# TensorE's task order in four planned stretches, taken from fixed permutations

## The chip, the cores and the metric

The kernel runs on one core of one Trainium2 chip. A core has a matrix engine (TensorE, in the profile PE for its matmuls and PEld for its weight loads), three engines for elementwise work (VectorE or DVE, ScalarE or ACT, GpSimd or POOL), and SyncE (SP), which here only issues the DMA transfers. Each engine runs its own instructions in the order in which they were issued, and waits on semaphores for the others. The metric is the device time of one execution in microseconds, the median of several runs.

## The reference

A two-layer encoder trunk is applied to two requests with shared weights: 256 and 512 tokens, each with the same 16 meta tokens in front, so 272 + 528 = 800 rows of 1024 numbers, all in float32. Layer 0 mixes tokens by multi-head latent attention, layer 1 by grouped-query attention in a window of 128 tokens with a sink logit for each head. Behind each follows a squared-ReLU MLP, and each of the four steps ends in a layer norm over a scaled residual:

```python
for i in range(DEPTH):                      # DEPTH = 2, DN_ALPHA = 4 ** 0.25
    mix = mla_mixer(h, ...) if i % 2 == 0 else gqa_mixer(h, ...)
    h = layer_norm(DN_ALPHA * h + mix, ln1_g[i], ln1_b[i])
    h = layer_norm(DN_ALPHA * h + sqrelu_mlp(h, mlp_w1[i], mlp_w2[i]), ln2_g[i], ln2_b[i])
return h[:, N_META:]

def sqrelu_mlp(x, w1, w2):                  # 1024 -> 4096 -> 1024
    h = jax.nn.relu(x @ w1)
    return (h * h) @ w2
```

`mla_mixer` has 16 heads with 64 plain and 32 rotated columns for queries and keys, and 64 for values; `gqa_mixer` has 16 query heads on 4 key heads of 64.

## The kernel before

Activations lie transposed, 128 of the 1024 features on the partitions and tokens along the free axis, in two halves of 400 tokens (`hf` 0 and 1; 384 of a half where the meta tokens are dropped). A float32 product is made of three matmuls: each operand is split into a rounded part (hi, by ScalarE) and the rest (lo, by VectorE), and `mm3` (lines 445 to 448) adds hi x hi, hi x lo and lo x hi in one PSUM bank. So each weight and each activation costs one ScalarE and one VectorE instruction before TensorE can use it. The MLPs use a seven-product scheme for blocks of two by two, whose sums of weights are made by VectorE or GpSimd (`weight_add`, line 1438).

After the input projection, which is written out in order, the work lies in four plans, built one after the other: attention 0 (`attention0`), MLP 0 (`mlp_middle` with l = 0), attention 1 (`attention1`) and MLP 1 (`mlp_middle` with l = 1). A plan is a list of tasks. Each has an engine, a planned cost in ns, a function that issues its instructions, what it reads and writes, and the buffers it holds (`Plan.task`). From them `Plan.order` makes the order in which all engines' instructions are issued:

- TensorE's tasks form a chain in the order in which the code writes them down: each depends on the one before (lines 238 to 240). That order is made by hand: which filling work stands between the scores of attention, how far transposes follow scores, and so on.
- For every task a latest start (`late`) is worked out back from the end, over dependencies and over buffers that have to come free, with `LAG` ns from one engine to another (190 behind TensorE, 70 behind VectorE and ScalarE, 90 behind GpSimd).
- `Plan.forward` then plays the plan forward: again and again it takes the task that can start first, or one on the same engine that is more urgent by `late`. For VectorE, ScalarE, GpSimd and SyncE this sets the order; for some sums it also chooses between GpSimd and VectorE (`ways`).
- Eight such rounds are made, each with `late` taken from the round before, and the round is kept whose last TensorE task ends first.

`Plan.issue` issues the tasks in the order of their planned starts. `plan.busy` says for how long other engines are still taken by the stretch before.

The two score banks of attention 0 (buffer `s`) are used in turn: `scores` (line 1045) fills one, VectorE takes the maximum (line 1060 or 1069), ScalarE the exponential (line 1064 or 1074), and then the bank is free. VectorE or GpSimd scales the result `p` (lines 1088 and 1091), `turn` (line 1110) transposes it on TensorE (line 1122), ScalarE copies it out (line 1129), `tmeta` does so for the meta keys (line 1139), and `avs` (line 1147) multiplies with the values. In attention 1 the same is done by `scores` (line 2185), `transposes` (line 2271; matmuls in lines 2283 and 2291, on the tiles `sma`), and `outputs` (line 2298). A layer norm is in three TensorE tasks: `mean`, `sums` (eight narrow matmuls, line 795 or 1524), then a square root on ScalarE and a reciprocal on VectorE (lines 799 and 800, or 1527 and 1528), and `scale` (line 805 or 1533), behind which VectorE and ScalarE scale and split the activations for what follows. In the MLPs `up_pair` and `down_group` write the products; each finished bank of a down product is added to `acc` by VectorE (line 1734). The last layer norm is in `end` (line 1875): `piece` writes the product and its addition (line 1906 or 1907), `norm` the statistics, the scaling and the output DMA.

The changed orders number TensorE's tasks of a plan from 0 as the code writes them down. The plans have 390, 360, 329 and 339 of them. Those that are spoken of below:

| plan | tasks |
|---|---|
| attention 0 | 7, 10, 13: the first scores (short request); 8 and 9: projections for the long request; 15, 18, 21, 24: scores of the long request; 16, 19, 22, 25: transposes (`turn`); 17 and 20: projections; 280, 328, 333: scores of the last two head pairs; 277, 279: `turn`; 282: a key projection; 305: first part of the output projection; 338, 339, 340: the last transposes; 341: the last `avs`; 342 to 349: parts of the output projection; 367, 370: `sums` and `scale` |
| MLP 0 | 1: `mean`; 8, 10 and 11: parts of up products; 9: `sums`; 12: `scale` |
| attention 1 | 14 and 16: `sums0` and `scale0`; 15: a down product that stands between; 33: `sums1`; 34: part of a query projection; 170, 171 and 178, 179: scores of block 5; 190 and 197: two transposes tasks on them; 175, 184: transposes and `outputs` of block 1 |
| MLP 1 | 1: `mean`; 9 and 12: `sums` and `scale`; 19 to 26: an up product in eight parts that follow the eight splits of the activations `hc`; 27 to 29: three up products; 32 to 34 and others: transposes of the residual; 327 to 338: `piece` |

## Time and profile before

| what | us |
|---|---|
| median of three runs | 1750.49 |
| lowest and highest | 1750.35 and 1751.98 |
| span of the profiled execution | 1750.74 |
| input projection, to TensorE's first planned task | 85.8 |
| attention 0, from TensorE's first task to that of MLP 0 | 373.5 |
| MLP 0 | 471.2 |
| attention 1 | 318.9 |
| MLP 1, to the last matmul's start | 493.2 |
| behind the last matmul | 8.1 |

The profiled execution's own time and the median differ by 0.25 us. The page of the profile gives each engine's busy time; the windows give the same for stretches of the span. A row of the timeline has a start (us from the span's start), a length, the engine and line, what is written and read, and, in brackets, how long the engine was idle before and what ended that. Consecutive instructions of one kind are merged with their count. A row of the waits names who waited for whom, the sum in us, how often, and the longest. Ends of matmuls are modelled: one starts before the one before it ends, so a busy TensorE isn't one at its peak.

### The profile page before, as it was taken

How to read it: one execution, taken by the hardware profiler on the slowest of the kernel's cores; microseconds unless marked ns; L12 is line 12 of the kernel's file. 1: busy time of each engine (PE TensorE's matmuls, PEld its weight loads, DVE VectorE, ACT ScalarE, POOL GpSimd, SP SyncE). 2: the span in 40 equal slices, each digit the busy share in tenths (PEclk: the TensorE clock that was granted, in tenths of full speed). 3: DMA queues.
4: the chain of work that ended last, by engine and by line, in shares of the span. 5: the costliest groups of instructions: out<-in, count | busy, mean ns of one | idle time of the engine just before them, and what ended most of it. 6: DMA issues, size and time to landing. Idle time of an engine off the chain costs nothing.

```text
span 1750.7 us, 28797 instructions
## 1 busy us (share of the span) xinstructions
PE 1732.5 (99%) x10806; PEld 1628.4 (93%) x10806; DVE 1448.0 (83%) x2937; ACT 1026.2 (59%) x2172; POOL 309.2 (18%) x290
## 2 busy tenths in 40 slices
PE   9999999999999999999999999999999999999998
PEld 9999999989999999999999998788989889988996
DVE  6998889886977898889876877876877888888877
ACT  5577777774655446545643627775665456545652
POOL 0011111112220111111103232332211111211110
PEclk9999999999999999999999999999999999999999
DMA  7211001114311221222122231021311222222222
GB/s 243 77 41 32 22 20 42 35 42 140 121 61 49 73 72 62 73 72 73 61 89 83 81 104 38 21 66 61 121 49 49 80 65 73 73 72 73 73 68 89
DMA packets 39453, 124.16 MB, mean 71 GB/s; under 512 B 4752, under 2 KB 9744, under 8 KB 39184
## 3 DMA queue, kind: packets, MB, share of 16 engines
q1 hardware_dynamic: 39312, 122.31, 21.3%
q8 instruction: 85, 1.39, 0.3%
q14 instruction: 56, 0.46, 0.1%
HBM read 119.15 MB, written 3.15 MB: 70 GB/s over the span
## 4 chain that ended last, share of the span: by engine, by line
PE 93%; DVE 4%; ACT 2%; issue 0%; DMA 0%; POOL 0%; SPq 0%; DVEq 0%; ACTq 0%
PE w L447 18%; PE w L448 18%; PE w L446 18%; PE wb L446 4%; PE wb L447 4%; PE wb L448 4%; PE wa L446 3%; PE wa L448 3%; PE wa L447 3%; PE wa L1155 2%; PE sa L446 2%; PE wa L1122 2%; PE wb L2309 2%; PE sa L448 2%; PE sa L447 2%; PE wb L2291 1%
## 5 line engine op out<-in xcount | busy, mean ns | idle before, releaser
L1734 DVE TENSOR_TENSOR acc<-acc,w 128x400 f32<-128x400 f32 (+1 forms) x306 | 184.3, 618 | 35.3 <-PE w L448 33.3
L1466 DVE TENSOR_TENSOR h<-sq,h 128x384 fp32r<-128x384 f32 (+1 forms) x164 | 94.6, 589 | 19.4 <-ACT h L1464 18.9
L446 PE MATMUL w<-h,wsp 128*128 128x400 f32 x316 | 108.9, 345 | 0.0
L447 PE MATMUL w<-h,wsp 128*128 128x400 f32 x316 | 108.9, 345 | 0.0
L447 PE MATMUL w<-h,wspi 128*128 128x400 f32 x316 | 108.9, 345 | 0.0
L446 PE MATMUL w<-h,wspi 128*128 128x400 f32 x316 | 108.7, 344 | 0.0
L448 PE MATMUL w<-h,wspi 128*128 128x400 f32 x316 | 108.7, 344 | 0.0
L448 PE MATMUL w<-h,wsp 128*128 128x400 f32 x316 | 108.6, 344 | 0.0
L1464 ACT CAST h<-sq 128x384 fp32r<-128x384 f32 (+1 forms) x164 | 82.5, 515 | 20.5 <-POOL sq L1472 19.3
L1091 POOL TENSOR_TENSOR p<-p,rs 106x512 f32<-106x512 f32 (+1 forms) x40 | 44.7, 1117 | 253.5 <-DVE pk L1082 162.2
L448 PE MATMUL w<-wspi,h 128*128 128x512 f32 (+1 forms) x182 | 71.6, 393 | 0.0
L446 PE MATMUL w<-wspi,h 128*128 128x512 f32 (+1 forms) x182 | 71.5, 393 | 0.0
L447 PE MATMUL w<-wspi,h 128*128 128x512 f32 (+1 forms) x182 | 71.5, 393 | 0.0
L1645 ACT COPY sq<-w 128x400 f32<-128x400 f32 (+1 forms) x72 | 35.0, 486 | 61.0 <-PE w L448 61.0
L1064 ACT ACTIVATE p<-sa,nm,rq 106x528 f32<-106x528 f32 (+1 forms) x80 | 63.4, 792 | 10.5 <-DVE nm L1061 4.5
L1060 DVE TENSOR_REDUCE nm<-sa 106x1 f32<-106x528 f32 (+1 forms) x80 | 56.3, 704 | 13.8 <-PE sa L448 12.4
L446 PE MATMUL w<-wsp,h 128*128 128x512 f32 (+1 forms) x170 | 67.1, 395 | 0.0
L448 PE MATMUL w<-wsp,h 128*128 128x512 f32 (+1 forms) x170 | 66.8, 393 | 0.0
L447 PE MATMUL w<-wsp,h 128*128 128x512 f32 (+1 forms) x170 | 66.7, 393 | 0.0
L446 PE MATMUL sa<-k,q 128*106 128x264 f32 (+5 forms) x208 | 63.8, 307 | 2.8 <-issue 0.9
L446 PE MATMUL w<-t,wsp 128*128 128x384 f32 (+1 forms) x176 | 60.0, 341 | 0.0
L448 PE MATMUL w<-t,wsp 128*128 128x384 f32 (+1 forms) x176 | 59.9, 341 | 0.0
(823 smaller groups left out, 6173.7 us busy)
## 6 DMA issues: line engine op xcount, KB each, us to landing
wrawo<-in_w_o_dram SPq DMA_DIRECT2D x32, 512.0 KB, 3.3
wraw0d<-in_w2b_dram SPq DMA_DIRECT2D x24, 512.0 KB, 3.3
wraw1d<-in_w2b_dram SPq DMA_DIRECT2D x18, 512.0 KB, 3.4
wrawq<-in_w_q_dram SPq DMA_DIRECT2D x8, 512.0 KB, 3.3
xr<-in_xT_dram SPq DMA_DIRECT2D x16, 200.0 KB, 3.4
wraw<-in_w_qn_dram SPq DMA_DIRECT2D x8, 384.0 KB, 3.1
wx1d<-in_w2b_dram SPq DMA_DIRECT2D x6, 512.0 KB, 3.2
out_dram<-fo SPq DMA_DIRECT2D x11, 256.0 KB, 2.0
```

Of the source, the lines that this page charges most:

```text
L446: nc.tensor.matmul(out, lh, rh, start=start, stop=False, **kw)
L447: nc.tensor.matmul(out, lh, rl, start=False, stop=False, **kw)
L448: nc.tensor.matmul(out, ll, rh, start=False, stop=stop, **kw)
L1060: plan.task("DVE", DVE(528), lambda: V.tensor_reduce(nm.t[:qm, 0:1], v(), axis=AX.XY, op=ALU.max, negate=True), reads=[ps], writes=[nm], n ...
L1064: lambda: S.activation(P_().rearrange("p (a b) -> p a b", b=264), v(), AF.Exp, bias=nm.t[:qm, 0:1], scale=sc, accum_out=rs.t[:qm, 0:1]),
L1091: f = lambda row=row, r=r, w=w: G.tensor_tensor(row()[:, META:T], row()[:, META:T], r().to_broadcast([qm, w]), ALU.mult)
L1122: nc.tensor.transpose(ps.t[:, k * qm : (k + 1) * qm], src[k], ident[:qm, :qm])
L1155: nc.tensor.matmul(av[64 * e : 64 * e + 64, :n], vt.t[:, k, h0 + 64 * e : h0 + 64 * e + 64], PT.t[:, e, k, :n], start=k == 0, stop=False, ...
L1464: plan.task("ACT", 530, lambda: S.copy(d.t[:, 0], c.t[:, :n]), reads=[c], writes=[(d, "hi")], new=[d])
L1466: "DVE", 570, lambda: V.tensor_tensor(d.t[:, 1], c.t[:, :n], d.t.bitcast(F32)[:, 0], ALU.subtract),
L1734: f = lambda: V.tensor_tensor(z, z, ps.t[:, : z.shape[-1]], ALU.add)
L2309: nc.tensor.matmul(av[64 * gi : 64 * gi + 64, :256], at["V"][:, kbs[k][0], gc : gc + 64], PT.t[:, a : a + 256], start=k == 0, stop=False, ...
```

## The change

TensorE's tasks keep what they do, and get another order: `ORDERS` has one permutation for each plan, by the numbers above, found beforehand by a local search. The chain of TensorE's tasks follows it. Against the order as written, 250 of 390, 308 of 360, 272 of 329 and 267 of 339 tasks stand at another place, by 1.3, 3.0, 2.3 and 2.2 places on average, and by 10, 24, 13 and 17 at most.

Three things go with it. Since a task can now depend on one with a higher number, the first `late` is worked out over a topological order in place of the numbers. Of the eight rounds that one is kept whose end is first, where an end now counts TensorE's last task and also the last task of each other engine, less a lead for each plan (`LEAD`; SyncE only where the lead is 0, in MLP 1). And in `end`, the small tiles of the last layer norm are made by whichever piece comes first. The orders of the other engines, and the issues of the DMAs, come from the same planner as before.

Of `ORDERS`, the lines that are spoken of below:

```diff
+import heapq
 import math
 from contextlib import ExitStack
 from types import SimpleNamespace
@@ -88,6 +89,51 @@
 DOWN_ORDERS = ((7, 1, 6, 5, 3, 4, 2), (1, 7, 6, 5, 3, 2, 4))
 
 
+ORDERS = [
+    "0 4 3 1 6 5 2 8-9 7 11-12 10 13-15 18 21 20 17 22 24-25 16 23 19 27 26 29 28 30 32-33 31 35 37 34 36 38-44 46-49 52 50-51 53 55 45"
...
+    "265-268 270 269 271 264 272-279 282 280-281 283 285-286 284 288 287 289 294 291-292 295 293 296 298 297 299-300 290 303 302 304 "
+    "301 308 307 306 305 313 310 309 315 311 314 317 316 318-319 312 320-321 323-326 322 327-330 332 331 334 337 333 336 338 335 339 "
+    "344 343 340 345 349 346 342 341 347-348 353 351-352 350 355 354 356-357 359-361 364 369 358 362 371 363 365-368 370 372 374-376 "
...
+    "0-1 5 2-4 10 6 11 7 9 8 12 15 13 16-17 19 18 20-21 14 22-25 29 26-28 30-31 36 33 37 41 32 39 34-35 46 38 40 45 47-48 53 50 43 49 "
...
+    "0-2 5 3-4 6-10 13 12 11 14 16-17 15 20 19 18 22 21 24 23 26 25 27-29 32 30-31 34 33 38 42 36 35 43-44 39 37 50-51 46 45 40 47 54 "
...
+    "178-179 177 174 180 183 175 181-182 184 186 185 190 188 187 191 196 192-194 197 195 189 199-203 198 207-208 210 209 205 211 206 "
...
+    "0-3 5 4 6-10 12 11 15-16 32 19 17 13 20-21 18 22 33 14 23-25 34 28-29 27 26 37 39 38 30 40 35 41 44 36 49-50 43 31 42 45 51-52 61 "
...
+    "309 313-314 319 316 308 320-321 315 324 322 318 323 317 326 325 327 329 328 330-331 333 332 335 334 337 336 338",
+]
+
+
+LEAD = (1400, 3000, 1400, 0)
+
+
 class Held:
 
 
@@ -102,10 +148,11 @@
 
     LAG = {"PE": 190, "DVE": 70, "ACT": 70, "POOL": 90, "SP": 0}
 
-    last = {}
+    last, count = {}, 0
 
     def __init__(self, bufs, own, in_turn=()):
         self.bufs, self.own, self.tasks, self.last, self.ways = bufs, own, [], {}, []
+        self.no, Plan.count = Plan.count, Plan.count + 1
 
         self.free = set(own) - set(in_turn)
         self.given = {tag: [] for tag in bufs}
@@ -162,7 +209,7 @@
 
 
         tasks, n = self.tasks, len(self.tasks)
-        line = [i for i in range(n) if tasks[i][0] == "PE"]
+        line = list(self.line)
         done, begin, places, took = {}, {}, [], {}
         ready = {i: 0.0 for i in range(n) if not deps[i]}
         wait = [len(d) for d in deps]
@@ -207,7 +254,7 @@
             e, cost, _ = self.ways[i][way[i]]
             held, port = tasks[i][4], tasks[i][5]
             if e == "PE":
-                line.pop(0)
+                assert line.pop(0) == i
             del ready[i]
             begin[i], done[i] = t, t + cost
             took[i] = way[i]
@@ -236,6 +283,10 @@
         tasks, n = self.tasks, len(self.tasks)
         deps = [set(t[3]) for t in tasks]
         line = [i for i in range(n) if tasks[i][0] == "PE"]
+        if ORDERS[self.no]:
+            ranks = [range(int(a), int(b or a) + 1) for a, _, b in (x.partition("-") for x in ORDERS[self.no].split())]
+            line = [line[k] for r in ranks for k in r]
+        self.line = line
         for a, b in zip(line, line[1:]):
             deps[b].add(a)
         after = [[] for _ in range(n)]
@@ -255,15 +306,28 @@
                 for i in users[id(x)]:
                     if i < k:
                         turns[i].append(k)
+        wait = [len(d) for d in deps]
+        heap = [i for i in range(n) if not wait[i]]
+        place = {}
+        while heap:
+            i = heapq.heappop(heap)
+            place[i] = len(place)
+            for k in after[i]:
+                wait[k] -= 1
+                if wait[k] == 0:
+                    heapq.heappush(heap, k)
+        assert len(place) == n
         late = [0.0] * n
-        for i in reversed(range(n)):
-            late[i] = min([late[k] - self.lag(i, k) for k in after[i] + turns[i]], default=0.0) - tasks[i][1]
+        for i in sorted(place, key=place.get, reverse=True):
+            later = [k for k in after[i] + turns[i] if place[k] > place[i]]
+            late[i] = min([late[k] - self.lag(i, k) for k in later], default=0.0) - tasks[i][1]
         first = min(late)
         late = [x - first for x in late]
         best = None
         for _ in range(rounds):
             begin, at, places, took = self.forward(deps, after, late)
-            end = max(begin[i] + tasks[i][1] for i in begin if tasks[i][0] == "PE")
+            ends = {e: max((begin[i] + self.ways[i][took[i]][1] for i in begin if self.ways[i][took[i]][0] == e), default=0.0) for e in self.LAG}
+            end = max(ends["PE"], *(ends[e] - LEAD[self.no] for e in ends if e != "SP" or not LEAD[self.no]))
             if best is None or end < best[0]:
                 best = (end, begin, at, took)
 
@@ -1900,7 +1964,7 @@
                 plan.task("PE", 12 * (229 if w == 512 else 119), run, reads=reads, writes=[ps], new=[ps])
 
                 def add():
-                    if i == 0:
+                    if not tl:
                         make()
                     if through:
                         return V.tensor_tensor(z[:, c], z[:, c], ps.t[:, :w], ALU.add)
@@ -2587,6 +2651,7 @@
 
     arrays = _layout({k: np.asarray(v) for k, v in inputs.items()})
     arrays.update(_constants())
+    Plan.last, Plan.count = {}, 0
     nc = bacc.Bacc("TRN2", target_bir_lowering=False, num_devices=1, dynamic_dma_scratch_size=1024)
     feed, ins = {}, {}
     for name, a in arrays.items():
```

## The prediction

> **What bounds the kernel now.** I read the page first, then the stretches between the four plans, then TensorE's waits, then the timeline around the longest of them.

> ```profile
> span 1750.7 us, 28797 instructions
> PE 1732.5 (99%) x10806; PEld 1628.4 (93%) x10806; DVE 1448.0 (83%) x2937; ACT 1026.2 (59%) x2172; POOL 309.2 (18%) x290
> ```

> ```profile
> core 0: us, PE busy (x) PEld busy (x) DVE busy (x) ACT busy (x) POOL busy (x), PEclk, DMA share, GB/s
> 0.00:85.70 85.70, 83.47 (x438) 82.52 (x439) 67.41 (x116) 50.42 (x94) 3.04 (x18) 1.00 0.48 162
> 85.70:459.20 373.50, 369.03 (x3044) 344.68 (x3043) 318.74 (x870) 266.26 (x658) 67.93 (x63) 1.00 0.17 54
> 459.20:930.40 471.20, 470.82 (x2588) 469.72 (x2587) 399.29 (x638) 254.08 (x457) 66.90 (x53) 1.00 0.21 70
> 930.40:1249.30 318.90, 316.69 (x2252) 288.42 (x2251) 243.58 (x652) 190.66 (x473) 98.44 (x100) 1.00 0.21 69
> 1249.30:1742.50 493.20, 492.37 (x2492) 443.04 (x2490) 413.90 (x650) 264.55 (x490) 72.88 (x56) 1.00 0.21 69
> 1742.50:1751.00 8.50, 0.09 (x1) 0.00 (x0) 5.06 (x13) 0.29 (x1) 0.00 (x0) 0.80 0.28 103
> ```

> The stretches are: input projection, attention 0, MLP 0, attention 1, MLP 1, and a tail after the last matmul. TensorE sets the end. Idle in the four planned stretches is 373.50 - 369.03 = 4.5, then 0.4, 2.2 and 0.8 us: 7.9 us in all. A new order of the same work can win only these, what each wait costs beyond its idle time, and a part of the tail. The two MLPs, 964 us of the span, have next to nothing to win.

> TensorE's waits, all that lie in these four stretches:

> ```profile
> PE sa L446 <- ACT p L1064: 1.3, 3, 0.5
> PE wb L795 <- DVE sqb L788: 1.3, 1, 1.3
> ...
> PE sa L446 <- issue: 0.9, 1, 0.9
> PE wb L2291 <- DVE sma L2266: 0.8, 2, 0.6
> ...
> PE wa L446 <- ACT pt L1129: 0.5, 1, 0.5
> PE sa L446 <- DVE q L924: 0.4, 1, 0.4
> PE w L447 <- DVE hc L1554: 0.3, 2, 0.2
> PE w L1507 <- DVE sqsum L2349: 0.3, 1, 0.3
> PE wa L1122 <- ACT acc L1181: 0.3, 1, 0.3
> PE wa L1139 <- ACT pt L1129: 0.2, 1, 0.2
> PE w L1524 <- DVE sq L1517: 0.2, 1, 0.2
> PE w L1507 <- DVE sqsum L1248: 0.2, 1, 0.2
> ```

> No row names a DMA: loads are never late for TensorE. A wait costs more than its idle time, because ends of matmuls are modelled and overlap the next start:

> ```profile
> 341.60 0.53 PE L1122 MATMUL wa<-ident,p 106*128 106x106 f32 x4
> 342.63 0.37 PE L446 MATMUL sa<-k,q 96*106 96x264 f32 x1 [0.51 <-ACT p L1064]
> ```

> ```profile
> 599.79 0.35 PE L446 MATMUL w<-t,wsp 128*128 128x400 f32 x1
> 599.98 0.35 PE L447 MATMUL w<-t,wsp 128*128 128x400 f32 x1
> ```

> A 400-column matmul lasts 0.35 us but the next starts 0.19 later, so some 0.2 us of delay can pass before idle time shows. Four transposes of 0.53 us would likewise let the next start some 0.3 us after 341.60; it came 1.03 after. The loss is 0.73 where the idle time is 0.51: I add 0.2 per wait.

> **The change, part by part.** It adds and removes no instruction; TensorE's tasks are permuted, and the other engines' orders and the DMA issues are planned anew around them. Sum of durations: no change. Single tasks now stand apart that stood together (transposes between matmuls); the rows above start at the usual spacing on such borders, so I take nothing. What counts is where a waiting task gets more work put ahead of it, and where one gets less. I number tasks as the orders do.

> *Attention 0, end.* The waits on p (three), pt (twice) and acc: 1.3 + 0.5 + 0.3 + 0.2 = 2.3 us idle, six waits, 3.5 us lost. Scores must wait until the bank of the scores two before is read: task 280 waited 0.51 with 1.4 us of work between (tasks 277 to 279 with one score of 0.73), so about 2.1 us are needed. The new order puts task 282 (0.8 us) ahead of 280; ahead of 328 the distance grows from 1.4 to 1.7; and ahead of the last avs (341) stand six tasks of the output projection that before came behind it. Won: 2.6 us (bounds 1.5 to 3.5).

> *Attention 0, start.* Task 7 waited 0.4 on q, task 18 0.9; with 0.2 each, and 0.3 at a transposition behind, 2.0 us lost. Tasks 8 and 9 (2.9 us) now stand ahead of 7: that goes. But 15, 18, 21 now follow one another, so between 15 and 21 lies one task of 0.73 us where 2.1 are needed: a new wait of 1.4 us. Won: 0.4 (bounds: 1.4 lost, 2.0 won).

> *Attention 1.* sums1 (task 33) lost 1.3 + 0.2 us; task 34 (six matmuls, 1.05 us) goes ahead of it and leaves 0.4 or less. Won 1.3 (1.0 to 1.5). The transposes behind sma lost 0.8 + 2 x 0.2, and 0.3 inside the group: 1.5 us. Task 197 now has 0.8 us more of TensorE's work between its own scores and itself, but 190 has 1.15 less, which only a new order on VectorE can make up: won 0.3 (0.5 lost to 1.5 won). On the other side the order is 14, 16: scale0 directly behind sums0, where a task of 2.2 us stood between. What lies between is this:

> ```profile
> 434.60 0.87 PE L795 MATMUL wa<-ones,sqa 128*100 128x1 f32 x8
> 435.50 0.26 ACT L799 ACTIVATE rsta<-wa,eps_ln 100x4 f32<-100x4 f32 x1 [0.94 <-PE wa L795]
> 436.07 0.17 DVE L800 RECIPROCAL rsta<-rsta 100x4 f32<-100x4 f32 x1
> ```

> From the last of the eight (ending 435.47) to the reciprocal's end at 436.24 are 0.8 us, about 1.0 against the usual spacing: a new wait of 1.0 (0.9 to 1.3). Everything of TensorE queues behind it. Five outputs tasks come 0.9 to 1.1 us behind the transposes that they read, where 5 us or more stood between; one ACT copy of a bank fits in that, if ACT is free at once (190.66 of 318.90 us busy). Lost 0.4 (0 to 1.5).

> *MLP 0.* sums (task 9) gets one more task ahead (1.1 us): its 0.2 + 0.2 goes. scale (12) has one task of 1.1 us behind sums instead of two.

> ```profile
> 469.52 0.87 PE L1524 MATMUL w<-ones,sq 128*100 128x1 f32 x8 [0.21 <-DVE sq L1517]
> 470.42 0.26 ACT L1527 ACTIVATE rst<-w,eps_ln 100x4 f32<-100x4 f32 x1 [0.39 <-PE w L1524]
> 471.65 0.17 DVE L1528 RECIPROCAL rst<-rst 100x4 f32<-100x4 f32 x1
> ```

> Here the reciprocal ended 1.4 us after the sums: with 1.1 us of cover 0.4 would show, unless VectorE's order brings it forward. Lost 0.2 (0 to 0.6). The same closer scale is in attention 0 (task 370) and in MLP 1 (12): 0.2 each. In down_group several parts now follow the part that used the same bank by 1.1 us instead of 1.6 to 3.3 (in MLP 1 by 1.4); between lies one VectorE accumulation:

> ```profile
> L1734 DVE TENSOR_TENSOR acc<-acc,w 128x400 f32<-128x400 f32 (+1 forms) x306 | 184.3, 618 | 35.3 <-PE w L448 33.3
> L1438 POOL TENSOR_TENSOR wraw0d<-wraw0d,wraw0d 128x512 f32<-128x512 f32 x12 | 15.5, 1290 | 156.8 <-DVE wsp L1427 80.9 <-DVE wspi L1427 62.0 <-issue 13.9
> ```

> 0.62 us fits in 1.1 with 0.2 to 0.3 for the hand-overs, if VectorE, 85% busy there, starts at once. Lost 0.4 in each MLP (0 to 3).

> *MLP 1.* Tasks 24 to 26 wait for the splits of hc:

> ```profile
> 1271.91 0.45 PE L446 MATMUL w<-hc,wsp 128*128 128x384 f32 x1
> ...
> 1275.12 0.34 PE L448 MATMUL w<-hc,wsp 128*128 128x384 f32 x1
> ```

> Eight intervals take 3.21 us; at 0.175 each they would take 1.40. Two transposes tasks (0.9 us) now stand ahead of 24, one between 25 and 26, and three slabs of 4.2 us ahead of 26. Won 1.6 (1.0 to 1.8). The mean of each MLP (task 1, 0.3 and 0.2 idle) keeps its place: nothing.

> *Tail.* The plan now also counts the other engines' ends, here SP's too.

> ```profile
> 1742.63 0.42 DVE L1906 TENSOR_TENSOR acc<-acc,w 128x256 f32<-128x256 f32 x1 [0.48 <-PE w L448]
> 1742.96 1.40 DVE L1916 BATCH_NORM_STATS2 fm<-acc 128x6 f32<-128x256 f32 x4
> ```

> One of the four statistics (0.35) fits into the 0.48 in which VectorE waited: won 0.3 (0 to 1.0).

> *Sum.* Won 2.6 + 0.4 + 1.3 + 0.3 + 0.4 + 1.6 + 0.3 = 6.9. Lost 1.0 + 0.4 + 3 x 0.2 + 2 x 0.4 = 2.8. Net 4.1 us. The profiled execution's span, 1750.7, is within 0.3 of the median 1750.49: **forecast 1746.4 us**. With all bounds at their good end: 3.5 + 2.0 + 1.5 + 1.5 + 0.4 + 1.8 + 1.0 = 11.7 won, 0.9 lost, so 1739.7. At their bad end: 1.5 - 1.4 + 1.0 - 0.5 + 0.4 + 1.0 = 2.0 won, 1.3 + 1.5 + 1.8 + 6 = 10.6 lost, so 1759.1.

> [...]

> **The rivals.**

> (a) *Full recovery.* All waits that have more work ahead of them go and the closer pairs cost nothing, because VectorE and ACT are planned to serve them: 11.7 won less the 0.9 that scale0 must cost: 1739.7. For it: the moves stand at the places where the waits are. Against: 15, 18, 21 and 14, 16 wait whatever the others do.

> (b) *Waits move.* What is won is spent on pairs that stand closer; 6.9 won, 3.5 to 9 lost: 1747.1 to 1752.6. For it: VectorE is 83% busy, and its work at the start of attention 0 is a queue, so a score issued earlier only waits longer.

> (c) *Slower: weights of the down groups come late.* The plan counts GpSimd's 512-wide sums at 185 + 1.67 x 512 = 1040 ns; the row above has 1290. An order without slack that relies on one such sum before each of six groups in two MLPs would wait 12 x 0.25 = 3 us; with the bank waits at their bad end (6) and the rest of the losses as above (2.0), 11 us against 6.9 won: 1754.6. It decides once the losses pass 6.9 + 3.5. Against: in 964 us of MLP no wait names a weight, so slack was there; and VectorE, which may take these sums, does when it is free earlier.

> (d) *It does nothing.* Hardly possible: the order is asserted in the plan. A plan that keeps all its waits would still give 1750.5.

> (e) *Hidden room behind the loads.* If time without a weight load were room, the four stretches would have 1656.8 - 1545.9 = 110.9 us of it, and the same share as above (4.1 of 7.9, 52%) would win 58: 1693. It needs matmuls that start late without idle time; the spacing of 0.19 us for 400 columns in MLP 0, at half of a matmul's own 0.35, shows none.

> **How the numbers follow.** A measurement of this kernel can tell about 0.2% (3.5 us) from no change. Chances: forecast 0.45 (1742 to 1748, of which 0.38 below 1747.0), (a) 0.17, (b) 0.28, (c) 0.08, (d) 0.01, (e) 0.01. Faster by over 0.2%: 0.38 + 0.17 + 0.01 + 0.02 of (b)'s edge = 0.58. Within: 0.34. Slower: 0.08. The range is from (a), 1739.5, to the upper part of (b), 1752.0; (c) and the far bad end stay out.

> **What would show it.** Same counts of instructions on every engine. At the end of attention 0 the waits on p, pt and acc fall below 1 us together; the wait on hc is gone; the one on sqb is below 0.5. New: a wait of about 1.4 at the third score of the first wide piece, one of about 1.0 at scale0 (named reciprocal) near 945 to 960. In the MLPs PE's idle time stays below 1 us; waits for accumulations or weights above 3 us there would make (c) right. If scale0 or 21 does not wait, VectorE's order matters more than I count, and (a) is near.

## The result, and the profile after

The changed kernel takes 1743.42 us (median of five executions, 1741.58 to 1744.29), the kernel before 1750.49 beside it: ratio 0.9950, 95% interval 0.9939 to 0.9961, 7.1 us less. The forecast was 1746.4, with a range of 1739.5 to 1752.0. Sign and range held; the account further down shows that the sum came out with a good deal of luck in its terms.

The page of the changed kernel, span and engines:

```profile
span 1741.6 us, 28738 instructions
PE 1726.0 (99%) x10806; PEld 1628.5 (94%) x10806; DVE 1432.8 (82%) x2921; ACT 1027.5 (59%) x2172; POOL 335.4 (19%) x306
```

TensorE does the same 10806 matmuls. VectorE has 16 instructions fewer and GpSimd 16 more, which the prediction had excluded ("adds and removes no instruction"): they are sums for which the plan may choose either engine (19 sums of weights went to GpSimd and 3 other sums to VectorE), and by the windows below 15 of VectorE's 16 fall into MLP 1. No wait names a weight, so rival (c) didn't come about.

The windows of the changed kernel, in the stretches that were shown of before (input projection, attention 0, MLP 0, attention 1, MLP 1, behind the last matmul):

```profile
0.00:84.00 84.00, 82.35 (x438) 81.31 (x439) 67.49 (x116) 50.48 (x94) 3.04 (x18) 1.00 0.49 165
84.00:455.00 371.00, 367.00 (x3044) 344.93 (x3043) 314.88 (x872) 264.97 (x659) 68.07 (x63) 1.00 0.17 54
455.00:927.10 472.10, 471.42 (x2586) 470.33 (x2587) 398.31 (x637) 254.94 (x459) 68.99 (x52) 1.00 0.21 69
927.10:1242.20 315.10, 313.87 (x2252) 288.87 (x2251) 240.54 (x653) 190.54 (x472) 96.56 (x100) 1.00 0.21 69
1242.20:1733.70 491.50, 491.29 (x2492) 443.08 (x2490) 406.82 (x635) 266.24 (x491) 98.73 (x73) 1.00 0.22 72
1733.70:1741.60 7.90, 0.08 (x1) 0.00 (x0) 4.73 (x12) 0.29 (x1) 0.00 (x0) 0.74 0.26 94
```

Read the lengths first (second number): attention 0 fell from 373.5 to 371.0, attention 1 from 318.9 to 315.1, MLP 1 from 493.2 to 491.5, while MLP 0 grew from 471.2 to 472.1. Idle time (length less PE busy) explains only part: attention 1 lost 1.0 us of idle time (2.2 to 1.2) and became 3.8 shorter. The input projection, whose program is the same, is 1.7 shorter as well; that lies in its first windows, and comes up at the end.

TensorE's waits in the changed kernel, all but two in the input projection (who waits, for whom, sum, times, longest):

```profile
PE sa L510 <- ACT p L1138: 2.9, 2, 2.4
...
PE w L510 <- DVE acc L1305: 0.8, 1, 0.8
PE wb L2355 <- DVE sma L2330: 0.6, 1, 0.6
PE wb L869 <- DVE rstb L864: 0.6, 1, 0.6
...
PE w L510 <- DVE acc L1798: 0.4, 1, 0.4
PE w L511 <- DVE h L1530: 0.2, 1, 0.2
PE w L1571 <- DVE sqsum L2413: 0.2, 1, 0.2
```

(Lines are 64 further down than before.) Gone are the waits on sqb, on hc, on q, and nearly all on p, pt and acc at the end of attention 0. There one of 0.56 us stands in the first row; it is at score 307, which didn't wait before, where before task 305 waited 0.51. New are a wait of 2.4 us at one score, one of 0.8 at MLP 0's first task, one of 0.6 at scale0 (`rstb`), and two in MLP 0's down groups (`acc`, `h`).

The largest, in the timeline of the changed kernel. Task 18, a score, waits until the bank of score 13 has been read:

```profile
104.86 0.71 DVE L1133 TENSOR_REDUCE nm<-sa 90x2 f32<-90x544 f32 x1
...
106.22 0.71 DVE L1124 TENSOR_REDUCE nm<-sa 106x1 f32<-106x528 f32 x1 [0.32 <-ACT q L813]
106.85 0.21 DVE L1134 TENSOR_SCALAR nm<-nm,rq 90x2 f32<-90x2 f32 x1
...
107.16 0.57 ACT L1138 ACTIVATE p<-sa,nm,rq 90x272 f32<-90x272 f32 x1
107.72 0.56 ACT L1138 ACTIVATE p<-sa,nm,rq 90x272 f32<-90x272 f32 x1
108.48 0.34 PE L510 MATMUL sa<-k,q 128*106 128x264 f32 x1 [2.37 <-ACT p L1138]
```

VectorE had the maximum of score 13 at 105.57 and came to its scaling only at 106.85, behind other instructions of its queue; ScalarE's exponentials followed, and TensorE stood still. What that did next is in the windows of 3.41 us around it, TensorE alone (length, PE busy, granted clock):

```profile
102.49:105.90 3.41, 3.41 (x30) 1.00 0.02 5
105.90:109.31 3.41, 1.04 (x9) 1.00 0.00 0
109.31:112.72 3.41, 3.41 (x18) 0.50 0.34 115
112.72:116.13 3.41, 3.41 (x31) 1.00 0.00 0
```

Behind a window in which TensorE was busy for 1.04 of 3.41 us, the granted clock is 0.50 for the next window: 18 matmuls where 30 went before. TensorE stood still for 2.4 us, and the half clock cost 1.5 more (e12 below).

### The profile page after: what moved, and what is told of

The parts are those of the page before. It is cut to its first block, busy times and chain, and to the rows that moved or that the text cites. A ratio compares the mean times of both kernels' runs of the same rounds, so it can differ in the third digit from the quotient of the medians.

```text
span 1741.6 us, 28738 instructions
## 1 busy us (share of the span) xinstructions
PE 1726.0 (99%) x10806; PEld 1628.5 (94%) x10806; DVE 1432.8 (82%) x2921; ACT 1027.5 (59%) x2172; POOL 335.4 (19%) x306
## 4 chain that ended last, share of the span: by engine, by line
PE 97%; DVE 2%; ACT 1%; issue 0%; DVEq 0%; POOL 0%; ACTq 0%; POOLq 0%
PE w L510 18%; PE w L511 18%; PE w L512 18%; PE wb L510 4%; PE wb L511 4%; PE wb L512 4%; PE wa L510 3%; PE wa L512 3%; PE wa L511 3%; PE wa L1219 2%; PE sa L510 2%; PE wa L1186 2%; PE sa L512 2%; PE sa L511 2%; PE wb L2373 2%; PE wb L2355 2%
## 5 line engine op out<-in xcount | busy, mean ns | idle before, releaser
L510 PE MATMUL w<-h,wspi 128*128 128x400 f32 x320 | 110.2, 344 | 0.8 <-DVE acc L1305 0.8
L511 PE MATMUL w<-h,wspi 128*128 128x400 f32 x320 | 110.3, 345 | 0.0
L512 PE MATMUL w<-h,wspi 128*128 128x400 f32 x320 | 110.2, 344 | 0.0
L1530 DVE TENSOR_TENSOR h<-sq,h 128x400 fp32r<-128x400 f32 (+1 forms) x167 | 102.2, 628 | 3.5 <-ACT h L1528 3.3
L1528 ACT CAST h<-sq 128x400 fp32r<-128x400 f32 (+1 forms) x167 | 84.3, 518 | 19.9 <-DVE sq L1536 10.9
L510 PE MATMUL w<-wsp,h 128*128 128x512 f32 (+1 forms) x176 | 69.5, 395 | 0.0
L512 PE MATMUL w<-wsp,h 128*128 128x512 f32 (+1 forms) x176 | 69.2, 393 | 0.0
L512 PE MATMUL w<-wspi,h 128*128 128x512 f32 (+1 forms) x176 | 69.1, 393 | 0.0
L510 PE MATMUL w<-wspi,h 128*128 128x512 f32 (+1 forms) x176 | 69.1, 392 | 0.0
L511 PE MATMUL w<-wspi,h 128*128 128x512 f32 (+1 forms) x176 | 69.1, 392 | 0.0
L511 PE MATMUL w<-wsp,h 128*128 128x512 f32 (+1 forms) x176 | 69.1, 392 | 0.0
L510 PE MATMUL w<-t,wspi 128*128 128x400 f32 (+1 forms) x180 | 61.5, 342 | 0.0
L512 PE MATMUL w<-t,wspi 128*128 128x400 f32 (+1 forms) x180 | 61.5, 342 | 0.0
```

The source lines that it names most:

```text
L510: nc.tensor.matmul(out, lh, rh, start=start, stop=False, **kw)
L511: nc.tensor.matmul(out, lh, rl, start=False, stop=False, **kw)
L512: nc.tensor.matmul(out, ll, rh, start=False, stop=stop, **kw)
L1528: plan.task("ACT", 530, lambda: S.copy(d.t[:, 0], c.t[:, :n]), reads=[c], writes=[(d, "hi")], new=[d])
L1530: "DVE", 570, lambda: V.tensor_tensor(d.t[:, 1], c.t[:, :n], d.t.bitcast(F32)[:, 0], ALU.subtract),
```

## The experiments

A stretch's length, from TensorE's first instruction of one plan to that of the next, repeats from run to run within 0.1 us as long as the orders in it are the same, the clock isn't halved, and a wait at its border stays on the same side of it. That makes it a far sharper measure than the median, and lets one kernel test a different thing in each stretch. The border matters for MLP 0: where its first task waits, the wait (0.9 us lost) is counted in attention 0, and MLP 0 itself is 0.4 shorter. As written it takes 470.8 us behind such a wait (e2, e9, e13) and 471.2 without (before, e1, e6, e8, e10); in the new order 472.1 behind it and 472.6 or 473.0 without (e4, e3). All lengths, from the traces ("task 44": from the plan's first instruction to that of attention 0's 45th task, behind which all of 0 to 43 are done in every order; the tail counts from the last matmul's start, where the table ahead of the prediction counts MLP 1 to that matmul's end, hence 493.2 and 8.1 there; the last column says for how many windows of 3.4 us the clock was halved in the profiled execution):

| run | attention 0 | MLP 0 | attention 1 | MLP 1 | tail | task 44 | halved |
|---|---|---|---|---|---|---|---|
| before | 373.51 | 471.20 | 318.88 | 492.97 | 8.42 | 48.30 | 0 |
| changed | 370.97 | 472.15 | 315.10 | 491.25 | 8.09 | 50.03 | 1 |
| e1_written_order | 373.50 | 471.20 | 318.86 | 492.97 | 8.42 | 48.30 | 0 |
| e2_attention_only | 372.26 | 470.80 | 315.04 | 492.90 | 8.41 | 51.34 | 2 |
| e6_few_moves | 370.79 | 471.20 | 318.66 | 492.11 | 8.43 | 48.40 | 0 |
| e3_start_as_written | 369.74 | 472.95 | 315.04 | 491.29 | 8.10 | 49.08 | 0 |
| e5_15_between | 371.05 | 472.09 | 315.43 | 491.29 | 8.09 | 50.02 | 1 |
| e8_one_move | 373.34 | 471.20 | 318.87 | 492.99 | 8.41 | 48.07 | 0 |
| e4_20_ahead_of_18 | 369.28 | 472.56 | 315.06 | 491.29 | 8.10 | 48.62 | 0 |
| e9_start_and_mlp0_as_written | 369.79 | 470.82 | 315.08 | 491.28 | 8.10 | 48.41 | 0 |
| e10_two_fillers | 369.84 | 471.25 | 314.88 | 491.28 | 8.09 | 48.42 | 0 |
| e11_parts | 371.86 | 470.95 | 318.38 | 491.05 | 8.41 | 48.30 | 0 |
| e12_changed_again | 369.43 | 472.08 | 315.02 | 491.27 | 8.09 | 48.54 | 0 |
| e13_transposes_alone | 369.51 | 470.82 | 318.88 | 491.33 | 8.10 | 48.07 | 0 |

**Is it the order, or the planner's new criterion?** All four permutations are left empty, which gives the order as written:

```diff
 ORDERS = [
-    "0 4 3 1 6 5 2 8-9 7 11-12 10 13-15 18 21 20 17 22 24-25 16 23 19 27 26 29 28 30 32-33 31 35 37 34 36 38-44 46-49 52 50-51 53 55 45"
...
+    "", "", "", "",
 ]
```

> The changed planner (its end criterion and first late) with TensorE's tasks as written in all four stretches. Theory A, the gain is in the order of TensorE's tasks: the four stretches keep their waits and their lengths between first tasks (373.5, 471.2, 318.9, 493.1) within 1 us each, at most 0.4 us of the tail goes, ratio 0.998 to 1.000. Rival B, the gain is in the other engines' orders, which the new criterion chooses: attention 1 is shorter by 2 us or more with its order as written, ratio 0.997 or below.

Median 1750.41, ratio 0.9998 (0.9989 to 1.0007). Every stretch, the tail too, has its length of before within 0.02 us. The gain needs the order (A): the new criterion by itself changes no stretch. The new order under the old criterion wasn't run.

**Do the stretches add up?** The MLPs get the order as written:

```diff
 ORDERS = [
...
-    "0-1 5 2-4 10 6 11 7 9 8 12 15 13 16-17 19 18 20-21 14 22-25 29 26-28 30-31 36 33 37 41 32 39 34-35 46 38 40 45 47-48 53 50 43 49 "
...
+    "",
...
-    "0-3 5 4 6-10 12 11 15-16 32 19 17 13 20-21 18 22 33 14 23-25 34 28-29 27 26 37 39 38 30 40 35 41 44 36 49-50 43 31 42 45 51-52 61 "
...
+    "",
 ]
```

> New orders in the two attentions alone, the MLPs as written. The changed kernel's profile has attention 0 2.5 us shorter, attention 1 3.8 shorter, MLP 0 0.95 longer, MLP 1 1.7 shorter than before. Theory A, the stretches add up: attention 0 and 1 as in the changed kernel within 0.5 us, MLP 0 near 471.2 but for the wait at its first task (0.9), MLP 1 near 493.1; so about 6 us less than before, ratio about 0.9965. Rival B, the MLPs' orders carry part of the attentions' gain over (their weights are loaded in the stretch before): attention 1 gains under 2.5 us.

Median 1743.87, ratio 0.9958 (0.9946 to 0.9971). Attention 1 has its new length to 0.06 us with MLPs as written around it, and MLP 1 that of before: the stretches add up (A). Attention 0 came out longer than in the changed kernel, and the windows of this run say why:

```profile
104.47:107.88 3.41, 1.49 (x13) 1.00 0.00 0
107.88:111.29 3.41, 2.97 (x14) 0.50 0.32 113
111.29:114.71 3.42, 3.42 (x17) 0.50 0.01 3
```

The same wait, but here the windows cut it so that the next one still holds 0.44 us without a matmul; the half clock lasts two windows, and task 44 is 1.3 us later than in the changed kernel.

**Do a few moves do it?** The order as written, with only the moves at the waits:

```diff
 ORDERS = [
+    "0-279 282 280-281 283 285-286 284 288 287 289 294 291-292 295 293 296 298 297 299-300 290 303 302 304 301 308 307 306 305 313 310"
...
+    "",
+    "0-32 34 33 35-328",
+    "0-23 32-33 24-25 34 27-29 26 30-31 35-338",
 ]
```

> The order as written but for the tail of attention 0 (from task 272 on as in the changed kernel), task 34 ahead of 33 in attention 1, and in MLP 1 two transposes tasks ahead of 24, one between 25 and 26, and tasks 27 to 29 ahead of 26. Theory A, a few waits hold most of the gain: the waits on p and pt at attention 0's end, on sqb and on hc go, which cost 3.6, 1.4 and 1.8 us; 6 us less, ratio about 0.9965, without the wait of 2.4 us at task 18 and without the one at scale0. Rival B, the gain is spread over many small spacings between tasks: at most 4 us less, ratio 0.9977 or above.

Median 1748.32, ratio 0.9979 (0.9970 to 0.9988). The lengths say 2.7 us in attention 0, as forecast for its end (2.6), but 0.9 in MLP 1 and 0.2 in attention 1. The wait at sums1 is still there:

```profile
PE wb L825 <- DVE sqb L818: 1.1, 1, 1.1
...
PE w L477 <- DVE hc L1584: 0.2, 1, 0.2
```

The second row is task 25 of MLP 1. It takes 1.05 us as before and 24 takes 1.09 (1.29 before); only 26, with three up products ahead of it, runs in 0.53. In the changed kernel 24 and 25 take 0.53 too, but there the parts 13, 14, 17 and 18 (4.3 us) also stand between 19 and 23, a move that the prediction doesn't name.

At sums1, task 34 ahead of it was to cover 1.05 us; the wait's end moved instead. From the stretch's first matmul (930.47 before, 925.66 here) VectorE's last addition for sums1 ends after 60.07 us before and after 60.94 here, by these rows of the two timelines:

```profile
977.42 2.17 POOL L2101 TENSOR_TENSOR ssb<-ssb,acc 128x400 f32<-128x400 f32 x2
979.62 1.19 DVE L2101 TENSOR_TENSOR ssb<-ssb,acc 128x400 f32<-128x400 f32 x2 [2.13 <-POOL ssb L2101]
...
989.96 0.57 DVE L788 TENSOR_TENSOR sqb<-sqb,sqb 128x400 f32<-128x400 f32 x1
```

```profile
972.14 3.29 POOL L2131 TENSOR_TENSOR ssb<-ssb,acc 128x400 f32<-128x400 f32 x3
975.47 1.18 DVE L2131 TENSOR_TENSOR ssb<-ssb,acc 128x400 f32<-128x400 f32 x2 [3.25 <-POOL ssb L2131]
...
986.03 0.57 DVE L818 TENSOR_TENSOR sqb<-sqb,sqb 128x400 f32<-128x400 f32 x1
```

With sums1 due later, the plan gives GpSimd one more of the sums `ssb` (three in a row for two); VectorE waits 3.25 us for them in place of 2.13, so that its additions to `ssb` begin 0.66 us later behind the stretch's first matmul, and that last addition ends 0.87 later. So of 1.05 us of cover 0.87 was given back. In the changed kernel it ends after 60.28 us, 0.2 later than before, and TensorE comes to sums1 only at 60.48, the 0.8 us lost at scale0 included:

```profile
986.86 0.58 DVE L852 TENSOR_TENSOR sqb<-sqb,sqb 128x400 f32<-128x400 f32 x1
```

By the sum, 3.8 us over the stretches, B's number held; A is right for the end of attention 0 alone.

**The start of attention 0.** Two repairs of the order around score 18, each an edit of the changed kernel:

```diff
...
-13-15 18 21 20 17 22 24-25 16 23 19 27 26
+13-25 27 26
...
```

> The changed kernel with tasks 13 to 25 of attention 0 in the order as written, so that 16 and 17 stand ahead of 18 again. Theory A, the two scores that follow at once are what waits: task 18 waits about 0.9 us in place of 2.4, TensorE's clock isn't halved behind it (that cost 1.7 us in the changed kernel's profile), and attention 0 is about 3 us shorter; the median falls by 1.5 to 3 us. Rival B, task 18 waits for VectorE, whose queue sets its start: then task 18 starts no earlier, what follows it starts as late as in the changed kernel but for the clock, and the gain is 1.7 us or less.

Median 1743.97, ratio 0.9954 (0.9942 to 0.9966). Score 18 waits 0.6 us, the clock stays at 1.0, and attention 0 is 1.2 us shorter than in the changed kernel, which is less than the half clock alone (1.5): rival B. The waits went to the tasks behind:

```profile
PE wa L1152 <- POOL p L1121: 1.1, 1, 1.1
...
PE sa L476 <- issue: 0.6, 1, 0.6
...
PE wa L1152 <- DVE p L1118: 0.5, 1, 0.5
```

```diff
...
-13-15 18 21 20 17 22 24-25 16 23 19 27 26
+13-16 20 18 17 19 21-25 27 26
...
```

> The changed kernel with the start of attention 0 in the order 13-16 20 18 17 19 21-25: a projection of 2.27 us more ahead of score 18. Theory A, the order of TensorE's tasks sets the waits: 18 doesn't wait, 24 waits 0.8 at most, the clock stays at 1.0 and task 44 starts 47.5 to 48.5 us behind the plan's first task (49.1 with the order as written from 13 to 25, 50.0 in the changed kernel). Rival B, VectorE's work up to there is a queue that is longer than TensorE's: the wait only moves to 24, 25 or later, and task 44 starts at 48.8 or later.

Median 1741.94, ratio 0.9946 (0.9932 to 0.9959). Task 44 at 48.62, between what the theories gave. With 2.27 us more of work ahead, score 18 still waits, inside itself, for VectorE's split of k. Where there was one wait of 2.4 us there are now three of 0.5 to 0.6 and one of 0.2:

```profile
PE sa L477 <- DVE k L781: 0.6, 1, 0.6
...
PE wa L1152 <- POOL p L1121: 0.6, 1, 0.6
...
PE wa L476 <- DVE q L781: 0.5, 1, 0.5
```

What this order wins over the changed kernel is the half clock and no more: where the changed kernel keeps its clock (e12) it reaches task 44 at 48.54. And behind both repairs MLP 0 takes longer (472.95 in e3, 472.56 in e4, 472.15 in the changed kernel), since the wait at its first task is gone from the end of attention 0 and its first tasks take 0.4 longer instead; in e3 a wait on `acc` is 0.4 longer too.

**Does the wait alone halve the clock?** In the order as written, score 18 goes ahead of the 1.7 us of work that covered its wait:

```diff
 ORDERS = [
+    "0-15 18 16-17 19-389",
+    "", "", "",
 ]
```

> The order as written in all four stretches, but for score 18 of attention 0 put ahead of tasks 16 and 17 (1.7 us). Theory A, the start of 18 hangs on VectorE and ScalarE: it waits 0.87 + 1.7 = 2.5 us, and TensorE, busy in less than half of one of the clock's 3.4 us windows, runs at half its clock for one or two windows (1.7 or 3.4 us lost); task 44 starts 1 to 4 us later behind the plan's first task than 48.3, more than a moved wait alone can cost (0 to 0.3, since 16 and 17 then fill later waits). Rival B, the half clock of the changed kernel had another cause: the clock stays at 1.0 and task 44 starts within 0.5 us of 48.3. [...]

Median 1752.01, ratio 1.0000 (0.9990 to 1.0009). A miss for A's premise: score 18 didn't wait 2.5 us; it began 2.6 us earlier than before, and waited 0.5 inside itself. Task 44 came 0.2 earlier. The reason is when VectorE takes the maximum of score 13, whose bank 18 needs; in the kernel before (first) and here:

```profile
108.36 0.72 DVE L1069 TENSOR_REDUCE nm<-sa 90x2 f32<-90x544 f32 x1
```

```profile
105.65 0.70 DVE L1099 TENSOR_REDUCE nm<-sa 90x2 f32<-90x544 f32 x1
```

From the plan's first task (85.76 and 85.44) that is 22.6 and 20.2 us. With 18 due earlier the plan moves the maximum forward in VectorE's queue. So a wait isn't a fixed distance between two tasks of TensorE; the other engines' orders are made anew around it, for better here and for worse in e6. The test says nothing on the clock; the next run does.

```diff
 ORDERS = [
     "0 4 3 1 6 5 2 8-9 7 11-12 10 13-15 18 21 20 17 22 24-25 16 23 19 27 26 29 28 30 32-33 31 35 37 34 36 38-44 46-49 52 50-51 53 55 45"
...
 ]
```

(No edit: the changed kernel, run again beside e10_two_fillers.)

> The changed kernel once more, beside the kernel with two fillers on the same chip. The stretches have the lengths of the first profile within 0.1 us (370.97, 472.15, 315.1, 491.25), but for the clock: if the half clock behind the wait at task 18 comes from one of the clock's windows of 3.4 us in which TensorE is busy in less than half, it shows again, for one window or two, as the windows fall, and attention 0 takes 371.0 or 372.3; without it attention 0 takes 369.3. The median is 1742 to 1744.5 us, and 2 to 4.5 above the kernel with two fillers.

Median 1743.13, ratio 0.9956 (0.9943 to 0.9970). Four stretches as before, the wait at score 18 too, but in this execution the clock's windows lay otherwise:

```profile
103.47:106.89 3.42, 2.48 (x21) 1.00 0.00 0
106.89:110.30 3.41, 1.98 (x16) 1.00 0.09 19
```

```profile
PE sa L476 <- ACT p L1104: 2.9, 2, 2.4
```

The 2.4 us fall into two windows, busy for 2.48 and 1.98 us, and the clock stays at 1.0. Attention 0 takes 369.43. So the new start costs 48.54 - 48.30 = 0.24 us for its wait, and the half clock 50.03 - 48.54 = 1.5 (or 51.34 - 48.54 = 2.8, e2) in those executions where it came. The times of the five executions (1741.5, 1741.6, 1743.1, 1743.2, 1744.8) don't show this by themselves: executions also differ by 1.7 us through their first windows, as the last section says.

**scale0 and sums1 in attention 1.**

```diff
...
-14 16-17 15 20
+14-17 20
...
```

> The changed kernel with task 15 of attention 1 (2.2 us) back between 14 (sums0) and 16 (scale0). Theory A, scale0 issued 2.2 us earlier is what lets VectorE begin the squares of the other half earlier, so the wait of 0.6 us at scale0 is the price of the missing wait at sums1: scale0 waits no longer, sums1 waits 0.8 us or more, attention 1 is 0.3 to 0.9 us longer than 315.1. Rival B, the two are separate: scale0 waits no longer, sums1 still doesn't wait, attention 1 is 0.75 us shorter (314.35).

Median 1743.49, ratio 0.9954 (0.9939 to 0.9970). scale0's wait is gone and attention 1 is 0.33 us longer, the amount A gave, but not in A's way: sums1 doesn't wait; two short waits on `hb` (the activations behind scale0) cost 0.4 and 0.5 more. Scaling and splitting of these activations starts later when scale0 does. The wait of 0.6 us at scale0 had been paid for already: without it, TensorE waits a little later for the same chain.

**The start and MLP 0 as written, the rest new.**

```diff
 ORDERS = [
-    "0 4 3 1 6 5 2 8-9 7 11-12 10 13-15 18 21 20 17 22 24-25 16 23 19 27 26 29 28 30 32-33 31 35 37 34 36 38-44 46-49 52 50-51 53 55 45"
+    "0-44 46-49 52 50-51 53 55 45"
...
-    "0-1 5 2-4 10 6 11 7 9 8 12 15 13 16-17 19 18 20-21 14 22-25 29 26-28 30-31 36 33 37 41 32 39 34-35 46 38 40 45 47-48 53 50 43 49 "
...
+    "",
...
 ]
```

> The changed kernel with tasks 0 to 44 of attention 0, and all of MLP 0, in the order as written. Theory A, these two stretches are where the search lost: task 44 starts at 48.3 us behind the plan's first task in place of 50.0, the clock isn't halved, attention 0 takes 368.3 to 369.7 us, MLP 0 470.8 to 471.3; with 315.1 and 491.3 that is 2.5 to 4 us less than the changed kernel's profile where it starts alike: ratio to the kernel before 0.993 to 0.9945. Rival B, what the start gains is lost behind it, because VectorE's queue is as long: attention 0 takes 370 us or more.

Median 1740.58, ratio 0.9938 (0.9926 to 0.9950), the fastest of all. Attention 0 at 369.79 lies just past the edge of A's range, 1.2 us below the changed kernel's first profile but 0.4 above its second, so of the start only the half clock is won. MLP 0 takes 470.82 against 472.08 and 472.15, all three with the wait at its first task: its new order costs 1.3 us, which is the sure part of the gain. From the plan's first task to the end the kernel takes 1655.07 us, the changed kernel 1655.89 where its clock isn't halved (e12) and 1657.56 where it is.

**Does more work ahead of a wait take its place?** Two moves on top of that kernel:

```diff
...
-304 301 308 307 306 305
+304 301 308 305 307 306
...
-186 185 190 188 187 191
+186 185 187 190 188 191
...
```

> The kernel with tasks 0 to 44 of attention 0 and all of MLP 0 as written, and two moves more, each a task that waits for nothing put ahead of one that waits: 305 (first part of the output projection, 1.1 us) ahead of score 307, which waits 0.6, and in attention 1 task 187 (1.05 us) ahead of the transposes 190, which wait 0.6. Theory A, work put ahead takes a wait's place: attention 0 is 0.5 to 0.8 us shorter than 369.8, attention 1 0.4 to 0.7 shorter than 315.1, 1 to 1.5 us in all. Rival B, the task moved brings work of VectorE or ScalarE along, or the wait shows up at the next task: under 0.3 us in each.

Median 1740.90, ratio 0.9945 (0.9933 to 0.9958). Attention 0 is 0.05 longer, attention 1 0.2 shorter: B. Work of 1.1 us was put ahead of a wait of 0.6 and the wait is as long as before, and 305, where it now stands, waits 0.3 itself. (These two lose 1.0 us, which attention 0 regains because MLP 0's first task no longer waits; MLP 0 is 0.4 longer for it.)

```profile
PE sa L476 <- ACT p L1104: 0.7, 1, 0.7
...
PE wb L2321 <- DVE sma L2296: 0.3, 1, 0.3
```

(The second is another task's: 190 no longer waits, and 197, some tasks later on TensorE, now does.)

**Which part of each order does it?** A closed part of the new order in each stretch:

```diff
 ORDERS = [
+    "0-44 46-49 52 50-51 53 55 45"
...
+    "272-389",
...
+    "0-29 32 30-31 34 33 35-328",
...
 ]
```

> One part of the new order in each stretch, the rest as written. Attention 0: tasks 45 to 271 in the new order; if what lies between the start and the end gains by small waits and spacings, it takes 371.5 to 372.2 us (373.5 as written); if the whole gain lies at its end, 373.0 or more. MLP 0: the new order up to the 154th task; if the two waits behind it (0.6 and 0.5 us) are all that the new order costs, 470.3 to 470.9 (471.2 as written, 472.15 in the changed kernel). Attention 1: 32 ahead of 30 and 34 ahead of 33, two moves; if what takes the wait at sums1 away is that the weights of 32 to 34 are split before the last squares, it takes 317.3 to 317.9 (318.9 as written, 318.66 with 34 ahead of 33 alone); if it needs more of the new order, 318.5 or more. MLP 1: the new order up to the 70th task; if all of its gain lies at the splits of hc, 491.2 to 491.6 (493.0 as written, 491.25 in the changed kernel).

Median 1746.66, ratio 0.9975 (0.9966 to 0.9984). Attention 0's middle wins 1.65 us by itself, as expected if small waits and spacings count. MLP 1's first 70 tasks win 1.9, more than the whole new order (1.7): its gain lies there. MLP 0, with its first 154 tasks in the new order, takes 470.95, 0.05 past the range given; what the new order loses lies behind them (257.9 us from there to the end, 259.4 in the changed kernel). Attention 1 wins 0.5 with the two moves, between the ranges; sums1 still waits 0.9.

**The transposes of block 5**, beside sums1 the largest gain of attention 1 in the changed kernel: from the start of 190 to the point where all tasks up to 197 are done it wins 1.8 us, or 1.1 with the new wait just before 190 (0.7) counted in.

```diff
 ORDERS = [
...
+    "0-186 190 188 187 191 196 192-194 197 195 189 199-203 198 207-208 210 209 205 211 206 212 204 213-328",
...
 ]
```

> Attention 1 as written but for tasks 187 to 212, which stand as in the new order: the four transposes on block 5 (189, 190, 197, 198), which stood within 8 us, are spread over 12. Theory A, this spreading alone takes their waits: attention 1 is 1.6 to 2.1 us shorter than 318.9 (in the changed kernel 1.9 of its 3.8 us are won between these tasks), and sums1 keeps its wait of about 1.3. Rival B, VectorE's maxima come in time only with the order of the whole stretch: 0.6 us or less. Attention 0: tasks 0 to 44 as written with 18 ahead of 16 and 17, the rest new; if the start and the rest add up, 369.3 to 369.8 (369.8 without that move, 0.3 won by it at the start). MLP 0 as written: 470.8 to 471.2. MLP 1 as in the changed kernel: 491.3.

Median 1746.06, ratio 0.9961 (0.9949 to 0.9974). Attention 1 takes 318.88, as before to 0.01 us: rival B. The waits on sma shrink from 0.8 to 0.2, and a new one, at 196, stands beside them:

```profile
PE wb L825 <- DVE sqb L818: 1.3, 1, 1.3
...
PE wb L2313 <- DVE pk L2284: 0.8, 1, 0.8
...
PE wb L2321 <- DVE sma L2296: 0.2, 1, 0.2
```

TensorE is 0.65 us ahead of the kernel before when task 197 is done, and 0.1 behind it fifteen tasks later. In attention 0 the start and the rest add up (369.51).

## Why the prediction was right, and where it was not

By its own terms, in us won. The measured numbers are differences between the two profiles at points where the same tasks are done.

| term | forecast | measured |
|---|---|---|
| attention 0, start (to task 44) | +0.4 | -1.7, of which -1.5 the half clock |
| attention 0, tasks 44 to 271 | 0 | +2.2 |
| attention 0, end, with scale | +2.4 | +2.1: +3.0, less 0.9 in front of MLP 0 |
| MLP 0 | -0.2 | -0.95 |
| attention 1 | +0.2 | +3.8 |
| MLP 1 | +1.0 | +1.7 |
| tail | +0.3 | +0.3 |
| sum | +4.1 | +7.4 |

- **End of attention 0: right.** The waits that were named went, by the moves that were named; e6 alone with that tail gives 2.7 in the stretch. One didn't go but moved: tasks 304, 305, 307 and 308 take 3.35 us in the kernel before and 3.45 in the changed one. The 0.9 us in front of MLP 0, where VectorE is late with the last bank, was not foreseen. It isn't fixed to this order: in e6, with the same tail, it is absent.
- **Start of attention 0: the step failed.** "15, 18, 21 now follow one another ... a new wait of 1.4" put the price at the third score; it fell on the second, and was 2.4, because 16 and 17 had covered 18. That the wait alone costs 0.24 us (e12) and that orders as different as those of before, e3, e4, e8 and e9 reach task 44 in 48.1 to 49.1 us shows what the step lacked: the start hangs on VectorE's queue and how the plan orders it (e8: score 13's maximum 2.4 us earlier by one move), more than on which task of TensorE stands there. The half clock wasn't in any term.
- **Middle of attention 0 and the spacings: the step failed.** "The rows above start at the usual spacing on such borders, so I take nothing." A task costs more in front of some kinds of task than of others: in the two profiles six 400-column matmuls of a projection in attention 1 take 1.09 us (median of 121) in front of another and 1.27 (13) in front of `outputs`, and 384 columns 1.05 (75) and 1.22 (17). Taking the two kernels' medians for each pair of kinds, borders account for 0.7 us of the gain in attention 1. In attention 0 and MLP 1 the figure hangs on how finely kinds are told apart, so it stays open there, and no border was tried alone. In the middle of attention 0 four score waits of 0.1 us idle (tasks 65, 110, 148 and 231), below what the list of waits shows, went too; they had cost 0.2 to 0.5 each, about 1 us of the 2.2. With the start as written ahead of it the same middle wins 1.5 (e11).
- **Attention 1: right by no merit of its terms.** It holds the largest error, +0.2 for +3.8. Between points where the same tasks are done it loses 0.75 us at scale0, wins 1.6 at sums1, 0.4 from there to block 5, 1.1 at that block's transposes and 1.4 behind them in small steps. scale0 waits as forecast (0.6 idle, 1.0 lost forecast), sums1 gained as forecast; but the gain of 1.3 was explained by "task 34 goes ahead of it", and with that move alone the stretch gains 0.2 (e6), with 32 as well 0.5 (e11), because the plan delays the squares. In the changed kernel, where sums1 doesn't wait, the time lost at scale0 is part of its cover. The transposes of block 5 gained 1.1 where 0.3 stood, and not by their own places (e13: 0.0). The losses put on the five `outputs` tasks and on the closer scales didn't show as waits. What the experiments settle is that the gain is not local at the places tried: five local edits, three on the order as written and two on the new one, gave -0.3 to +0.5. In the changed kernel the scores on block 5 begin earlier than before by 1.5 us (task 170) and 3.6 us (178), so VectorE can begin their maxima earlier; that this is the cause is argued from the trace and wasn't tried alone.
- **MLP 0: right in kind.** The first twelve tasks won 0.85 (0.4 forecast for sums; 0.36 of it only because a wait stands in front of the stretch instead: as written they take 13.31 us, and 12.95 behind that wait in e9). The bank waits, 0.4 forecast with an upper bound of 3, came to 1.1 in two places (`h` 0.5, `acc` 0.6); all that lies behind the first twelve tasks lost 1.8, of which 0.7 isn't located. e9 and e11 show that the order as written there is better.
- **MLP 1: the waits were right, the moves only in part.** The waits on hc went: 1.9 us won in the first 70 tasks, 1.6 forecast; 0.2 was lost behind them, 0.4 forecast. But the moves to which the prediction gave the 1.6 win 0.86 when made alone (e6). The rest comes with the new order of the first 70 tasks (e11); that it is 13, 14, 17 and 18 between 19 and 23 is argued from the trace and wasn't tried alone.
- **Tail: right,** 0.33 us; by the order (e11, with a tail as written, has 8.41), not by the criterion (e1).
- **Rival (b)** was the better description in three of the places tried: at the start of attention 0, at sums1 and at the transposes, waits did move. It lost because they moved less than was won elsewhere. Rival (e) is off by 50 us.

So the mechanism held where TensorE's own distance to a wait was the limit (end of attention 0, hc), and failed where VectorE's queue was. The largest term, attention 1, is half of the gain, and its cause stays open.

## What to carry to other kernels

A wait of the bounding engine goes with more work ahead of it only if the engine that is late keeps its order: look at its queue in the microseconds before the wait, and where a plan makes that order, expect it to spend the slack that the move gives it (0.87 of 1.05 us at sums1). Where TensorE keeps catching up with VectorE's queue, a local move can be worth nothing (318.88 us for 318.88). Compare stretches between two points of the trace rather than medians: they repeat to 0.1 us where the waits at their borders are the same, and show a change that pays in one stretch and costs in another, which can then be left out (MLP 0 as written: 470.8 for 472.1 us).

## What the hardware showed

**The first windows differ from one execution to the next.** Windows of TensorE at the start, before and changed:

```profile
6.77:10.19 3.42, 3.42 (x12) 1.00 0.98 299
10.19:13.60 3.41, 3.41 (x21) 1.00 1.05 395
```

```profile
3.50:6.91 3.41, 3.40 (x11) 1.00 0.83 258
6.91:10.32 3.41, 3.41 (x20) 1.00 0.98 325
```

11 or 12 matmuls in a window become 20 or 21, in the changed kernel at 6.91 us and in the kernel before only at 10.19: 400-column matmuls start every 0.33 us ahead of that, every 0.18 soon behind it. (The first record of the granted clock is at these same points, 6.91 and 10.19; what the clock was ahead of it is not shown.) The first plan began at 84.0 us in the changed kernel and at 85.8 in the kernel before. Of the fourteen profiles ten have that start at 83.6 to 84.0 us, and four (before, e3, e8, e13) at 85.4 to 85.8. So 1.7 of the 9.1 us between the two profiled spans isn't the change's, and the executions of one kernel fall into groups: of 21 of the kernel before, 7 lie at 1750.2 to 1750.6, 13 at 1752.0 to 1752.7, and one above. (In e1's profiled execution, of 1750.59 us, the first plan began at about 83.9 us, in e8's, of 1752.12, at 85.4.) An execution's time is also 1.7 to 1.9 us longer than its span (1743.47 for 1741.6; once, in e13, 2.35), which the prediction and the text ahead of it took as the same: the profiled execution of the kernel before, with a span of 1750.74, by this took about 1752.5 and is one of the later group, not within 0.25 us of the median.
